# Copying a matrix with its four quadrants exchanged: one DMA per 64 rows with runs of 16 KB, in place of two with runs of 8 KB

## The chip, the cores and the metric

The kernel runs on one core of a Trainium2 chip. The metric is the device time of one execution in microseconds (us). The kernel before was timed three times: median 811.06 us, from 810.79 to 811.39.

The core has five engines with their own instruction queues (PE, DVE, ACT, POOL, SP) and 16 DMA engines that move data without them. The profile abbreviates SP's queue as SPq.

## The reference

```python
def setup_inputs():
    return {
        "x": np.random.randn(8192, 8192).astype(np.float32),
    }

def reference(x: np.ndarray) -> np.ndarray:
    return np.fft.ifftshift(x)
```

For even sizes `ifftshift` moves every element by half the matrix in both directions: `out[r, c] = x[(r + 4096) % 8192, (c + 4096) % 8192]`. The four quadrants of the matrix change places across the diagonal. Nothing is computed. A row has 8192 floats of 4 bytes, 32 KB; half a row is 16 KB and is contiguous in both matrices. The matrix has 268.4 MB, which must be read once and written once.

## The kernel before

There is no tile in the core's memory: every DMA copies straight from the input tensor in HBM to the output tensor in HBM. The helper `both` issues one such DMA on a given queue. It takes `rows` output rows from `row` on, and of each row two pieces of `piece` floats: one at column `col` in the left half, one at the same place in the right half, `hc` = 4096 floats further on. Both pieces come from the same input row, `hr` = 4096 rows away; the left piece of the output is read from the right half of the input (the middle dimension of the input pattern steps by `-hc`). So the order inside the DMA is row by row, and in each row the left piece of the output, then the right one.

The loop at the end of the function goes over the matrix in blocks of `rows = ENGINES * apart` = 64 rows. The outermost dimension of the DMA's pattern has these 64 rows, and the 16 DMA engines share them, four consecutive rows (`apart`) each. For every block there are two DMAs, one for each `col` in `(0, piece)` with `piece = hc // 2` = 2048 floats: the first copies the first 8 KB of either half of the rows, the second the last 8 KB. A DMA moves 1 MB; 128 blocks make 256 DMAs, all issued on SP's queue in the order of the loop. Within one DMA an engine has 4 rows x 2 pieces = 8 contiguous runs of 8 KB.

No two DMAs touch the same output bytes, and none reads what another wrote, so no DMA depends on another. The framework gives each DMA a semaphore that its 16 engines count up when their share has landed, and there are eight of these in turn: before it issues a DMA, SP waits until the one issued eight earlier has landed. At the end SP waits for the last ones.

Of the kernel before, what the change touches and what calls it, by code (L numbers as in the profile page):

```python
# [1 line left out]

# [4 lines left out]


ENGINES = 16  # L10


@with_exitstack
def kernel(
    ctx: ExitStack,
    tc: tile.TileContext,
    x: bass.AP,
    out: bass.AP,
):
    nc = tc.nc  # L20
    R, C = x.shape
    hr = R // 2
    hc = C // 2

    def both(queue, row, col, rows, piece):

        queue.dma_start(
            out=bass.AP(out.tensor, out.offset + row * C + col, [[C, rows], [hc, 2], [1, piece]]),
            in_=bass.AP(
                x.tensor,  # L30
                x.offset + (row + hr) % R * C + hc + col,
                [[C, rows], [-hc, 2], [1, piece]],
            ),
        )


    apart = 4
    piece = hc // 2
    rows = ENGINES * apart
    for row in range(0, R, rows):  # L40
        for col in (0, piece):
            both(nc.sync, row, col, rows, piece)


# [1 line left out]
_INS = ['x']  # L46
_OUTS = [((8192, 8192), 'float32')]


def kernel(**inputs):  # L50
    import numpy as _np
    import concourse.bacc as _bacc
    import concourse.tile as _tile
    from concourse import mybir as _mybir
    from concourse.bass_utils import run_bass_kernel_spmd as _run

    nc = _bacc.Bacc("TRN2", target_bir_lowering=False, num_devices=1)  # L57
    arrays, args = {}, []
    for name in _INS:
        a = _np.ascontiguousarray(inputs[name])  # L60
        if a.dtype.kind in "iu":
            a = a.astype(_np.int64)
        arrays[f"in_{name}_dram"] = a
        args.append(nc.dram_tensor(f"in_{name}_dram", a.shape, _mybir.dt.from_np(a.dtype), kind="ExternalInput").ap())
    for i, (shape, dtype) in enumerate(_OUTS):
        dt = _mybir.dt.from_np(_np.dtype(dtype))
        args.append(nc.dram_tensor(f"out_{i}_dram", shape, dt, kind="ExternalOutput").ap())
    with _tile.TileContext(nc) as tc:
        kernel(tc, *args)
    r = _run(nc, [arrays], core_ids=[0])  # L70
    got = tuple(r.results[0][f"out_{i}_dram"] for i in range(len(_OUTS)))
    return got[0]
```

## Time and profile before

| | |
|---|---|
| median of three runs | 811.06 us |
| the profiled execution | 810.44 us |
| its span, first to last instruction | 808.7 us |
| DMA instructions (line 27, SP) | 256 of 1024 KB |
| median time from a DMA's issue to its landing | 25.1 us (from 6.0 to 26.0) |
| time of one DMA instruction on SP | 562 ns, the longest 682 |
| first and last issue | 0.7 and 783.1 us |
| busy time of POOL, the only engine with any | 0.2 us, four memsets |

The profile comes from one execution; its time lies 0.6 us below the median of the three timed runs. Besides the page, the trace holds a record of each DMA packet: when it started, how long it took and its size, though not on which engine it ran. A rate in GB/s counts the bytes once, while each is read and written; the page's figure for HBM counts both directions.

### The profile page before, as it was taken

The page shows a single profiled execution, that of the slowest core. Times are in us where ns is not written, and L with a number is a line of the kernel's source. Part 1 is how long each engine was busy: PE and PEld are TensorE (multiplying, and loading weights), DVE is VectorE, ACT ScalarE, POOL GpSimd, SP SyncE. Part 2 cuts the span into 40 slices and gives each one's busy share as a digit, 9 for nine tenths or more (in the row PEclk, how much of TensorE's full clock was granted, in tenths as well). Part 3 has the DMA queues.
Part 4 walks back from the last instruction along what each step waited for, and adds up shares of the span by engine and source line. Part 5 has one row for each costly group of instructions (what it writes and reads, how often), then busy time and mean ns, then how long its engine had stood idle before and what let it go on. Part 6 is the DMA issues. An engine that isn't in the chain of part 4 may idle for free. (4 is left out here: it accounts for less than half of the span.)

```text
span 808.7 us, 301 instructions
## 1 busy us (share of the span) xinstructions
POOL 0.2 (0%) x4
## 2 busy tenths in 40 slices
POOL 0000000000000000000000000000000000000000
DMA  8999999999999999999999999999999999999998
GB/s 301 331 335 329 336 334 330 335 332 336 332 335 334 336 331 334 339 328 335 331 335 339 334 334 337 331 336 330 336 334 331 339 332 334 333 336 331 337 335 294
DMA packets 36866, 268.47 MB, mean 332 GB/s; under 512 B 4096, under 2 KB 4096, under 8 KB 4096
## 3 DMA queue, kind: packets, MB, share of 16 engines
q1 hardware_dynamic: 36864, 268.45, 99.3%
q14 instruction: 2, 0.02, 0.0%
HBM read 268.44 MB, written 268.44 MB: 664 GB/s over the span
## 5 line engine op out<-in xcount | busy, mean ns | idle before, releaser
L57 POOL MEMSET const-bfloat16-1.0<- 128x1 bf16 x1 | 0.1, 102 | 0.0
L57 POOL MEMSET const-uint8-127<- 128x1 uint8 x1 | 0.1, 102 | 0.0
L57 POOL MEMSET const-float32-1.0<- 128x1 f32 x1 | 0.1, 99 | 0.0
L57 POOL MEMSET const-float32-0.0<- 128x1 f32 x1 | 0.1, 98 | 0.2 <-issue 0.2
## 6 DMA issues: line engine op xcount, KB each, us to landing
out_dram<-in_x_dram SPq DMA_DIRECT2D x256, 1024.0 KB, 25.1
```

The costliest lines, as they stand in the source:

```text
L57: nc = _bacc.Bacc("TRN2", target_bir_lowering=False, num_devices=1)
```

## The change

The loop over the two column pieces goes away. Each block of 64 rows is copied by one DMA whose pieces are the whole halves: `col` is 0 and `piece` is `hc` = 4096 floats. A contiguous run is 16 KB in place of 8 KB, a DMA moves 2 MB in place of 1 MB, and there are 128 DMAs in place of 256. The number of runs that an engine has in one DMA stays at eight, and so do the order of rows and halves, the queue, the rows that an engine takes and the eight semaphores.

```diff
     apart = 4
-    piece = hc // 2
     rows = ENGINES * apart
     for row in range(0, R, rows):
-        for col in (0, piece):
-            both(nc.sync, row, col, rows, piece)
+        both(nc.sync, row, 0, rows, hc)
```

## The prediction

> **What bounds the kernel now.** I read the page's queue table first, then SP's waits, then the busy table of chosen stretches of the span, and last the single packet records of the trace (start, length and size of each). No compute engine does anything but four memsets at the start, and the chain of waits ends with them after 0.4 us, so it says nothing here: everything is in the DMA queue.
>
> ```profile
> span 808.7 us, 301 instructions
> ...
> DMA packets 36866, 268.47 MB, mean 332 GB/s; under 512 B 4096, under 2 KB 4096, under 8 KB 4096
> ## 3 DMA queue, kind: packets, MB, share of 16 engines
> q1 hardware_dynamic: 36864, 268.45, 99.3%
> q14 instruction: 2, 0.02, 0.0%
> HBM read 268.44 MB, written 268.44 MB: 664 GB/s over the span
> ```
>
> Of 36,864 packets 4,096 are under 512 B: 16 for each of 256 DMAs, the semaphore packets (4 B in the records). The other 32,768 carry 268.44 MB, 8192 B each, one contiguous run of the code. Their time fills 99.3% of the 16 engines: no engine idles for want of work. SP confirms it:
>
> ```profile
> SPq L27 <- DMA out_dram<-in_x_dram: 634.0, 248, 3.2
> ```
>
> 256 DMAs less 248 waits: SP keeps 8 in flight and waits for the oldest before each further one. So the issue is no limit. The question left is whether the engines or the memory behind them set the pace:
>
> ```profile
> core 0: us, POOL busy (x), PEclk, DMA share, GB/s
> 4.00:5.40 1.40, 0.00 (x0) 1.00 1.03 433
> 8.00:12.00 4.00, 0.00 (x0) 1.00 1.01 344
> 20.00:780.00 760.00, 0.00 (x0) 1.00 1.00 334
> 804.00:805.40 1.40, 0.00 (x0) 1.00 0.99 404
> ```
>
> The last column is what one direction moved. The same engines, as busy as later, moved 433 GB/s in the first DMA, 344 a little later and 334 for the rest. They can do more than they are let do, and what holds them back builds up within microseconds. In the packet records the shortest usual packet takes 309 ns, and on its engine the next begins 3 to 4 ns before it ends: a period of 306 ns, or 428 GB/s for 16 engines, the rate of the first DMA. From 20 us on, 62% of the packets take this floor; the mean is 391 ns. Summed, an engine's data packets take 800.8 us, of which 168 us lie above the floor. I call that part stall. The limit is shared, behind the engines, and shows as stall.
>
> Is stall tied to the packet boundary? By following each engine's chain of packets (matched by their times, so a few links may be wrong) I get the mean stall by place in a DMA, packets 1 to 8 (four rows, right half of the input then left): 91, 73, 77, 86, 90, 75, 76, 88 ns. The first packet behind a semaphore is no worse than the others, so there is no cost per DMA. But 1, 4, 5 and 8 average 88.7 and the others 75.3: which half of which row is read matters to the memory. And stall is not independent from packet to packet: behind an unstalled packet the mean is 105 ns, behind one stalled by 300 to 500 ns it is 14. While one packet is held, the next, of the other half, comes in.
>
> **The change, part by part.** The profiled execution took 810.44 us, 0.62 under the median 811.06. It consists of 2.18 us to the first packet, 805.35 to the end of the last, 1.13 to the end of the span, and 1.78 outside it. The change issues 128 DMAs in place of 256, each an engine's 8 data packets of 16 KB instead of 8 KB, over the same rows in the same order; bytes are the same.
>
> Issue: 128 DMA instructions fewer on SP (median 562 ns each), and 120 waits in place of 248. SP has no other work. I cost this at nothing: the 7 DMAs queued behind the one that runs hide it, and they now hold twice the bytes. Without that cover the saving would be on the path, at most 128 x 0.56 = 72 us; the 99.3% rules that out. Landing should go from 25.1 to about 50 us, which delays nobody.
>
> Fixed cost of packets: the nearest row is the semaphore packet, 4 B, 9 ns with 3 ns overlapped, so 6 ns for almost no data. Each engine has 1024 data and 128 semaphore packets fewer: 1152 x 6 = 6.9 us at most. At least it is nothing, if the memory hands out its bytes at 334 GB/s whatever the engines spare. As a majority of packets runs at the engine's floor, but the total is held at 334, I take half: -3.5 us.
>
> The Trainium skill ("DMA: Bandwidth & Descriptors", section "Why small descriptors are slow") gives a packet about 3 cycles of fixed overhead inside the engine and counts it as important for packets of 256 B; by it, at the 850 MHz of its bandwidth section, the data packets save 1024 x 3.5 ns = 3.6 us where engines set the pace. The trace's 6 ns agrees in kind.
>
> End: the engines' last packets end between 805.5 and 807.5 us. Twice the granule can stretch that by as much again; 0 to +2 us, I take +1.
>
> Stall: an engine now stays 612 ns instead of 306 in one half before it alternates. The trace has no 16 KB packet, so I bound the term. Upper end: the relief by a neighbour from the other half is gone, and each 8 KB is stalled like one behind an unstalled packet: (105 - 82) x 2048 packets = +47 us. Lower end: longer runs suit the memory and all packets come down to the better places: (75.3 - 82) x 2048 = -13.7 us. The nearest row is the spread by place, +-6.7 ns or +-13.7 us, since what doubles is the stay in one place. I give it the positive sign, as held packets are now relieved by the other half only after 16 KB; and half its size, because reading ahead goes on. That it goes on can be seen at the start: a first packet took 1058 ns, 749 over the floor, the next 309 at once, so at 306 ns a packet about 2.4 packets (20 KB) were already under way. This reach covers 2.4 packets now and 1.2 of 16 KB. Term taken: +6.9 us.
>
> Sum: 810.44 - 3.5 + 1 + 6.9 = 814.8 us; against the median, 811.06 + 4.4 = 815.5.
>
> **Rivals.** *No change.* The memory sets 334 GB/s whatever the run length: 811, from 809.4 to 812.7 (0.2% either way is about what a measurement here can tell). For it: the flat rate in the 38 inner slices of the page (328 to 339), and no stall tied to the boundary. Against it: stall depends on half and neighbour, which the change touches. If the hardware cuts a run of 16 KB into packets of 8 KB, the change does not do what it says and also ends here, at most 0.8 us (128 semaphore packets) faster.
>
> *Faster.* Each 16 KB block is now visited once, where before its second 8 KB came a DMA (3.1 us) later. If stall per byte stays as it is, the whole 6.9 us show: 804.2. If in addition the memory keeps the 344 GB/s of the stretch from 8 to 12 us, 268.4 MB take 780 instead of 804 us: 787. For it: 344 and 433 were reached. Against: it was lost again by 20 us with no change in the code's pattern.
> "HBM Reference" of the Trainium skill (section "Specifications (TRN2)") gives 716 GB/s for the stack; by it this copy of 537 MB could not end under 750 us, an estimate, and the 664 of the page leaves 7%. The first DMA's 2 x 433 lies above that figure for 1.4 us.
>
> *Much slower.* If not even the next packet of 16 KB can be read ahead, each pays its latency: 612 + 749 = 1361 ns, x 1024 = 1394 us, some 1399 in all. The point from which it decides: with one packet read ahead a period would be 749 ns, 350 GB/s, still over 334, so it decides only when reading ahead holds less than one full packet. Against it: the 20 KB under way seen above.
> One rule speaks for it: the Trainium skill's "DMA: Bandwidth & Descriptors" ("Latency and other measured facts", on row pitch) has HBM to HBM copies of rows of 16 KiB at 214 GB/s a direction at best. By it the copy would take 1254 us, about 1259 with the ends; this trace, at 8 KB, moves 334, and none here shows 16 KB.
>
> **Chances.** Forecast, somewhat slower (over 812.7): 0.44. No change: 0.14. Faster (under 809.4): 0.37, of which about 0.07 lies below 793. Much slower: 0.05. Predicted time 815.5. Cases of both signs hold most of the chance: the forecast's own range is 812.7 to 845 (0.05 of the forecast's case lies above, towards +47). The range 793 to 845 leaves out 0.07 + 0.05 + 0.05. Faster 0.37, same 0.14, slower 0.44 + 0.05 = 0.49.
>
> **What would show it.** 16,384 data packets and 2,048 semaphore packets on the queue; floor about 610 ns (two floors less one fixed cost); under 35% of the packets at the floor (35% of today's pairs of neighbours have no stall) and a mean over 2 x 391 = 782 ns; GB/s between 20 and 780 us about 331; SP's waits 120. A mean under 776 ns shows the faster rival, first packets far over 1.4 us that repeat later the much slower one. Wrong would be the sign above all: if both 8 KB halves of a block are cheap together for the memory, the stall term is negative.

## The result and the profile after

The changed kernel takes 814.01 us (median of 6 runs, 813.39 to 814.80). The kernel before took 810.90 us in the 6 runs of the same comparison. The ratio is 1.0038, 95% interval 1.0027 to 1.0048: slower by 3.1 us, where 4.4 were forecast. The profiled execution took 813.94 us.

First the queue table of the changed kernel:

```profile
span 812.2 us, 173 instructions
...
DMA packets 18433, 268.45 MB, mean 331 GB/s; under 512 B 2048, under 2 KB 2048, under 8 KB 2048
## 3 DMA queue, kind: packets, MB, share of 16 engines
q1 hardware_dynamic: 18432, 268.44, 99.5%
...
HBM read 268.44 MB, written 268.44 MB: 661 GB/s over the span
```

2,048 semaphore packets and 16,384 data packets, so a run of 16 KB is one packet, and the rival in which it is cut does not hold. The engines are as full as before (99.5%). They are full for longer.

SP's waits (for whom, us in total, times, longest):

```profile
SPq L27 <- DMA out_dram<-in_x_dram: 686.8, 120, 6.8
SPq L66 <- DMA out_dram<-in_x_dram: 49.0, 4, 31.0
```

120 waits, on average 5.7 us where 2.6 were before; the median landing went from 25.1 to 50.5 us. As reckoned, that idles no engine: the engines stay full.

The stretches, in the same columns as in the prediction (the last is GB/s in one direction):

```profile
core 0: us, POOL busy (x), PEclk, DMA share, GB/s
4.00:5.40 1.40, 0.00 (x0) 1.00 1.00 386
8.00:12.00 4.00, 0.00 (x0) 1.00 1.00 340
20.00:780.00 760.00, 0.00 (x0) 1.00 1.00 332
804.00:805.40 1.40, 0.00 (x0) 1.00 0.98 328
```

Here the time went: 332 in place of 334 GB/s over the long middle. That is 0.6%, to be read with its rounding; on 804 us it would be 3 to 5 us. By the packet records the middle 96% of the bytes take 3.2 us longer, so the ends hardly matter.

The packet records say what an engine's 807.0 us of data packets are made of. The floor is 611 ns for 16 KB, where two packets of 8 KB took 618; the mean is 788 ns, where two took 782. Above the floor lie 181.4 us an engine in place of 168.0. So the floors fell by 7 us of packet time, and stall rose by 13. Not all of the 7 us is engine time: each packet still begins 3 to 4 ns before the one ahead of it ends, so one data packet fewer spares its engine some 3.6 ns and not 7, 3.7 us in all. The experiments ask what these numbers mean.

### The profile page after: what moved, and what is told of

It is laid out like the page before. It is cut to its first block, busy times and chain, and to the rows that moved or that the text cites. A ratio compares the mean times of both kernels' runs of the same rounds, so it can differ in the third digit from the quotient of the medians.

```text
span 812.2 us, 173 instructions
## 1 busy us (share of the span) xinstructions
POOL 0.2 (0%) x4
## 2 busy tenths in 40 slices
DMA packets 18433, 268.45 MB, mean 331 GB/s; under 512 B 2048, under 2 KB 2048, under 8 KB 2048
## 3 DMA queue, kind: packets, MB, share of 16 engines
q1 hardware_dynamic: 18432, 268.44, 99.5%
## 6 DMA issues: line engine op xcount, KB each, us to landing
out_dram<-in_x_dram SPq DMA_DIRECT2D x128, 2048.0 KB, 50.5
```

## The experiments

The first four ran on a chip on which the kernel before takes 823.5 us, the later ones on two chips with 810.5 and 811.1. Ratios are to the kernel before on the same chip, with 95% intervals. The expectations speak of three theories: S (the engine's stay in one half of a row makes the stall), W (the size of a DMA does) and P (the length of a packet does).

**16 KB runs in small DMAs.** One row for each engine, 512 KB, 512 DMAs; each engine copies the same runs in the same order as in the changed kernel. (The trace does not say on which engine a packet ran; which rows an engine takes is read from the access pattern.)

```diff
-        both(nc.sync, row, 0, rows, hc)
+        for one in range(apart):
+            both(nc.sync, row + one, [apart * C, ENGINES], hc)
```

(The helper takes the outermost dimension in place of a number of rows.)

> 16 KB runs as in the changed kernel, each engine with the same runs in the same order, but 512 DMAs of 512 KB (one row an engine) in place of 128 of 2 MB, so 4 MB in flight in place of 16. Theory S (the engine's stay in one half of a row, 16 KB, makes the stall): the DMA's size does not matter, about 814 us plus 384 more semaphore packets an engine at 6 ns, up to 2.3 us: 814 to 817. Rival W (the larger DMA, its 16 MB in flight or its coarser end cost the 3 us): 811 or under, with the stall per 16 KB back from 177 ns to about 164. Rival P (the packet's length itself): as S, 814 to 817.

Measured: 823.71 us, 1.0001 (0.9991 to 1.0011). As a ratio, that is what W expected, and under the range of S and P.

**The changed kernel's order in packets of 8 KB.** 128 DMAs of 2 MB; of each half the second 8 KB first, then the first.

```diff
-    out [[C, rows], [hc, 2], [1, piece]]   in [[C, rows], [-hc, 2], [1, piece]]
+    out [[C, rows], [hc, 2], [-piece, 2], [1, piece]]   in [[C, rows], [-hc, 2], [-piece, 2], [1, piece]]
```

(Shorthand: the access patterns alone. `piece` is 4096 floats in the first line and 2048 in the second, where both sides also start `piece` further on.)

> The changed kernel's 128 DMAs of 2 MB and its stay of 16 KB in one half of a row, but in two packets of 8 KB (the second 8 KB of a half first, so that the runs are not joined). Theory S (stay in one half): the stall of the changed kernel and the fixed cost of 1024 more packets an engine, 814 plus 0 to 6 us: 814 to 820. Rival P (a packet of 16 KB, whatever its place): 810 to 812, as before. Rival W (size of the DMA): 814.

Measured: 824.18 us, 1.0005 (0.9997 to 1.0014). As a ratio, that is what P expected; S and W expected about 1.004 or more.

**Alternating packets of 8 KB in DMAs of 2 MB.** The kernel before with `apart = 8`.

> Packets of 8 KB that alternate between the halves as in the kernel before, but DMAs of 2 MB (128 rows, 8 rows to an engine), so 16 MB in flight as in the changed kernel. Theory S and rival P: 810 to 811.5, as before, the 128 semaphore packets fewer worth at most 0.8 us. Rival W: about 814. The engines stand 8 rows apart in place of 4, which none of the theories counts.

Measured: 823.04 us, 0.9991 (0.9982 to 1.0000). That fits S and P and not W. It is 1.1 us less than the run before, which has the same packets and the same size of DMA in the changed order.

**Alternating packets of 4 KB.** The kernel before with `piece = hc // 4` and four columns.

> Packets of 4 KB that alternate between the halves, 512 DMAs of 512 KB. Theory S: half the stay of the kernel before, so stall per byte goes down by about as much as it rose from 8 to 16 KB (13 us), against the fixed cost of 2048 more data and 256 more semaphore packets an engine at 6 ns, 13.8 us if all of it shows: 798 to 812. Rival P: the fixed cost alone, 811 to 825. Rival W: smaller DMAs, 808 to 811.

Measured: 845.58 us, 1.0257 (1.0232 to 1.0282), 22 us slower. All three expectations failed. The stretches of this kernel:

```profile
8.00:12.00 4.00, 0.00 (x0) 1.00 1.08 231
12.00:20.00 8.00, 0.00 (x0) 1.00 1.02 276
20.00:40.00 20.00, 0.00 (x0) 1.00 1.03 300
40.00:60.00 20.00, 0.00 (x0) 1.00 1.03 308
60.00:100.00 40.00, 0.00 (x0) 1.00 1.02 325
```

A slump at the start, which takes until 60 us to pass, and then 322 to 325 GB/s up to 780 us, where the 8 KB kernels of this chip have 328 and 329. So a shorter stay in one half is not better in itself, or its gain is smaller than what 4 KB costs; the two can't be told apart here.

The first three contradict each other: one fits W alone, one P alone, one S and P. What they say stayed unclear, because the changed kernel had not run on that chip, and packets are held longer on it. The floor of a packet is the same there, but the alternating 8 KB packets of 2 MB DMAs have a mean of 398.3 ns, and 393.5 on one of the other chips. So the changed kernel was run again beside two of them.

**The changed kernel again**, on the chip with 810.5 us.

> The changed kernel once more, beside the two below on one chip, since the former experiments ran on a chip on which the kernel before takes 823.5 us and not 811. If the 0.38% belong to the kernel, the ratio is again 1.003 to 1.005; if they belong to the first chip, 0.999 to 1.001. Theories S and P say the first, and so does W.

Measured: 814.11 us, 1.0035 (1.0022 to 1.0047). The loss is there on a second chip, so it is the kernel's.

**16 KB runs in small DMAs, again.**

> 16 KB runs in 512 DMAs of 512 KB once more, now beside the changed kernel. Theories S and P: like the changed kernel, within 0.1% of it. Rival W (16 MB in flight make the difference): like the kernel before, ratio 0.999 to 1.001, with the changed kernel at 1.003 to 1.005.

Measured: 812.47 us, 1.0017 (1.0006 to 1.0027), between the theories: a smaller loss than the changed kernel's, despite 384 more semaphore packets for each engine. On one chip, with the same runs in the same order on each engine, the size of the DMA alone moves the time by 1.6 us (814.11 to 812.47).

**The changed order in packets of 8 KB, again.**

> The changed kernel's order and DMAs, its 16 KB in two packets of 8 KB, once more, now beside the changed kernel. Theory S: like the changed kernel, ratio 1.003 to 1.006. Rival P: like the kernel before, 0.999 to 1.001.

Measured: 814.67 us, 1.0041 (1.0027 to 1.0056). From the page of this kernel, and its long stretch:

```profile
DMA packets 34817, 268.45 MB, mean 330 GB/s; under 512 B 2048, under 2 KB 2048, under 8 KB 2048
```

```profile
20.00:780.00 760.00, 0.00 (x0) 1.00 1.00 332
```

34,817 packets less 2,048 semaphore packets and one of instructions are 32,768 of 8 KB. This speaks strongly against rival P. Packets of 8 KB, floor 309 ns, and a loss as large as the changed kernel's is there. It needs no packet of 16 KB; the order of the bytes or the size of the DMA is enough for it. (Within a half the second 8 KB now comes first, which no theory counts, so this run does not show what the changed kernel's own order costs in packets of 8 KB.)

**The kernel before again**, for its trace on this chip.

> The kernel before, for a profile of it on the chip of these runs: ratio 1, and if the chip's memory is what differs from the first chip, the same floor of 309 ns and a higher mean than 391 ns.

Measured: 810.14 us in one run, mean packet 391.7 ns at the same floor, as on the first chip (391). Its stretch:

```profile
20.00:780.00 760.00, 0.00 (x0) 1.00 1.00 334
```

Against it the 8 KB kernel with the changed order has 4.2 us more stall an engine (177.6 against 173.4, both counted from 307 ns) with equal packets. This surplus is no sign of the order: the next run alternates like the kernel before, in DMAs of 2 MB, and has 177.3.

**Alternating 8 KB in DMAs of 2 MB, again**, on the chip with 811.1 us, as the last three.

> Packets of 8 KB that alternate between the halves, in DMAs of 2 MB over 128 rows, once more, to compare with the runs on a chip where the kernel before takes 811 us. Rival W (DMAs of 2 MB, 16 MB in flight): ratio 1.003 to 1.005, like the changed kernel. Theory S (two stretches of 8 KB of one half in succession, in one packet or in two): 0.999 to 1.001, like the kernel before. If the chip is again the one of 823 us, 0.998 to 1.000 as there, and W is then weaker by one more run only.

Measured: 812.26 us, 1.0016 (1.0007 to 1.0024). Neither expectation: DMAs of 2 MB have a part of the loss, about 0.16 of the 0.4%. Its stretch:

```profile
20.00:780.00 760.00, 0.00 (x0) 1.00 1.00 333
```

Where that part comes from is open; the run also sets the engines 8 rows apart.

**16 KB runs in DMAs of 1 MB.** The changed kernel with `apart = 2`.

> 16 KB runs, left and right half in succession, in DMAs of 1 MB as in the kernel before (32 rows, engines 2 rows apart in place of 4). Rival W: 0.999 to 1.001. Theory S: 1.003 to 1.005. Between them, 1.001 to 1.003, if both have a part, as the 512 KB DMAs with 1.0017 let suspect.

Measured: 813.75 us, 1.0035 (1.0023 to 1.0047). A DMA as large as in the kernel before, and all of the loss. By itself it speaks for S and against W.

**Alternating 8 KB in DMAs of 512 KB.** The kernel before with `apart = 2`, the control of the run above.

> Packets of 8 KB that alternate between the halves, in DMAs of 512 KB (32 rows, engines 2 rows apart), so 4 MB in flight in place of 8. Rival W: less in flight is better, so 0.996 to 0.999 less the 256 more semaphore packets (up to 1.5 us): 0.996 to 1.001. Theory S: 1.000 to 1.002, the semaphore packets alone. It is also the control for the engines' distance of the run before it.

Measured: 813.42 us, 1.0027 (1.0016 to 1.0038). Above S's range, and it weakens the run before it: at 2 rows apart, 8 KB runs lose too. 256 more semaphore packets at 6 ns would be 1.5 us of its 2.2, if all of it showed. Beside this control the 16 KB runs cost 0.08% more, less than the intervals can tell. Less in flight does not help, which is against W. The trace can't say where the time went, since the profiled execution was the fastest of the seven (811.11 us) and as quick as the kernel before:

```profile
20.00:780.00 760.00, 0.00 (x0) 1.00 1.00 334
```

**16 KB runs, one half per DMA.** An engine copies four left halves, then four right halves.

```diff
-        both(nc.sync, row, 0, rows, hc)
+        for half in (0, hc):
+            one(nc.sync, row, half, rows)
```

> 16 KB runs, but a DMA of 1 MB takes the left half of 64 rows and the next the right half: an engine copies four left halves, then four right halves. If the relief comes from the other half of the row (theory S as the prediction has it), an engine now stays four packets in one half: 1.006 or more. If only the two stretches of 8 KB in succession count, 1.003 to 1.005. Rival W (DMA of 1 MB): 0.999 to 1.001.

Measured: 819.12 us, 1.0107 (1.0084 to 1.0130), as theory S said. But its trace says when:

```profile
8.00:12.00 4.00, 0.00 (x0) 1.00 0.92 291
...
20.00:210.00 190.00, 0.00 (x0) 1.00 1.00 324
210.00:400.00 190.00, 0.00 (x0) 1.00 1.00 330
400.00:590.00 190.00, 0.00 (x0) 1.00 1.00 332
590.00:780.00 190.00, 0.00 (x0) 1.00 1.00 332
```

The kernel loses in the first 400 us, most of it in the first 200. From 400 us on it has 332 GB/s, no less than the changed kernel. A plausible reading is that the engines, which start together in the same half, drift apart and then cover both halves among them; the runs did not test it. What the trace shows is that a stay of four packets costs nothing beyond that of one from 400 us on.

The runs of 8 and 16 KB together, as ratios:

| | packets | DMA | engines apart | chip of 823.5 us | chips of 810.5 and 811.1 us |
|---|---|---|---|---|---|
| changed kernel | 16 KB | 2 MB | 4 rows | not run | 1.0035 |
| its runs in small DMAs | 16 KB | 512 KB | 4 rows | 1.0001 | 1.0017 |
| its runs in DMAs of 1 MB | 16 KB | 1 MB | 2 rows | not run | 1.0035 |
| changed order | 8 KB | 2 MB | 4 rows | 1.0005 | 1.0041 |
| alternating | 8 KB | 2 MB | 8 rows | 0.9991 | 1.0016 |
| alternating | 8 KB | 512 KB | 2 rows | not run | 1.0027 |
| one half per DMA | 16 KB | 1 MB | 4 rows | not run | 1.0107 |

No single theory fits them all. In DMAs of 2 MB the changed order costs more than alternation, by 1.1 us on one chip and by some 2 us between the others; the size of the DMA moves the time by about as much (1.6 us with 16 KB runs, 1.3 us with alternating 8 KB). The distance of the engines changed along with the size of the DMA in three of the runs and was never varied alone, so it is a rival that stands untested. The three kernels that ran on both kinds of chip lose 0.16 to 0.36% less on the slow one, and why is open too. None of the kernels is faster than the one before beyond the intervals.

## Why the prediction came out, and where its terms were wrong

The sign, the size and the place were right: somewhat slower, 0.38% against a forecast of 0.54%, through a rate in the middle of 332 against a forecast of 331 (by the prediction's own sum it should have said nearly 333). The marks were met: 120 waits, a floor of 611 ns (about 610), 32% of the packets at it (under 35), a mean of 788 ns (over 782). The bound was read rightly: the memory's pace, not the engines'. That the sum came so near is in part luck. The prediction itself gave slower 0.49 and faster 0.37, and the errors of its terms cancel: counted in engine time, both the saving (3.5) and the stall (6.9) were too small, as the traces have 9 to 10 and 13.4 us; counted in what the kernel's time shows, both were too large.

**What bounds the kernel.** Borne out. The slower chip has the same floor and more stall, so what differs between the chips lies behind the engines; and twice as many packets for the same bytes did not cost time, as the point on fixed cost shows.

**Issue, nothing.** Right. The landings doubled and the engines stayed at 99.5%.

**Fixed cost of packets, -3.5 us.** Wrong in size, and this is the step that failed most clearly. The price was too high: a data packet fewer spared its engine 3.6 ns (618 - 611 = 7 less the lost overlap) and not 6. And the time did not show even that. The changed kernel and the same order in packets of 8 KB, on one chip, differ by 1024 data packets an engine and by 0.6 us (814.11 and 814.67); the ratios 1.0035 and 1.0041 carry some 0.0013 each, so up to about 2 us may hide there, 3.5 hardly. Their traces (profiled executions of 814.65 and 814.67 us) show the exchange: the kernel with 8 KB packets spends about 4 us more of an engine on fixed cost and 5 more in gaps, has 9 us less stall (173.5 against 182.9), and from the first packet to the last both take 809.5 us. "If the memory hands out its bytes at 334 GB/s whatever the engines spare", the lower end, was the nearer one: what an engine spared came back as stall. The prediction had the evidence (16 engines that could move 428 and are let move 334) and still took half.

**End, +1 us.** No such cost was found. The last packets end within 1.6 us, where 2.0 were before (1.4 and 1.1 in the traces of the chip with 810.5 us). In its place stands a cost of the 2 MB DMAs that the prediction did not have: 1.3 us by the run with alternating 8 KB (0.6 to 1.9), in the steady rate (333 against 334, to be read with the rounding) and not at the end. Its cause is open, and the smaller DMAs do not line up with it: the 16 KB runs lose least at 512 KB, the 8 KB runs lose at 512 KB too, with the engines 2 rows apart.

**Stall, +6.9 us.** Right in sign, wrong in size, and its reason is not shown. The changed order in DMAs of 2 MB, at equal packets, costs 3.3 us (1.0041); less the 1.3 of the large DMAs some 2.0 are left for the order, with an uncertainty of about 1.5, from runs on two chips. The pair on the chip with 823.5 us gives 1.1. The 13 us by which stall rose are mostly the engines' savings given back as waiting: about 5 us of fixed cost (data and semaphore packets, less the lost overlaps) and 4.6 us less of gaps between packets (8.3 to 3.7 us an engine, by the chains). What is left, about 4 us, is the time that the kernel lost (3.5 us from the first packet to the last in these two traces). And the row that the size was taken from, the spread by place in a DMA, does not carry over: in the changed kernel the places 1, 4, 5 and 8 average about 177 ns of stall, and 2, 3, 6 and 7 about as much. That an engine is relieved by the other half stays unproved: four packets in one half ran at 332 like one, from 400 us on. Whether it is the alternation that helps, or the return to a block a DMA later, was not separated. An order of 8 KB packets that alternates and comes back two packets later was not tried.

**The rivals.** Much slower: excluded, 16 KB packets are read ahead (an unstalled packet lasts 611 ns, and 32% do). The rule of the Trainium skill ("DMA: Bandwidth & Descriptors", "Latency and other measured facts"), 214 GB/s a direction at best for HBM to HBM copies of 16 KiB rows, was measured with rows 512 KiB and more apart and does not carry over to this copy, whose rows lie 32 KB apart: 332. Faster: stall per byte did not stay as it was, and the 344 GB/s were again lost by 20 us (340 between 8 and 12 us). No change: the flat rate that spoke for it was real, but the rate itself moved, from 334 to 332.

## What to carry to other kernels

When 16 busy DMA engines together move less than their own floor allows, do not expect fewer or longer packets to pay: here the time saved in the engine reappeared as stall (the changed kernel and its order in twice as many packets took 814.1 and 814.7 us). The shortest packet and the rate of the first microseconds tell the two limits apart. To learn whether a longer run or its order costs, cut the long run into short packets and keep the order as far as the pattern allows; here that run had the whole loss without the long packet. And run the changed kernel beside the experiments on the same chip: without it the first three runs here could not be read.

## What the runs showed of the hardware

- Two chips of the same kind differ by 1.5% on this copy (medians of the kernel before, 823.5 us against 810.5 and 811.1), more than any of the orders of 8 and 16 KB tried moved it (1.1% at most).
- With 16 data packets for each engine in a DMA, SP did not wait for landings inside the loop (line 27) at all; the DMA instruction itself took long. Its only waits for DMAs in the run of alternating 8 KB in 2 MB DMAs come at the end:

```profile
SPq L68 <- DMA out_dram<-in_x_dram: 35.8, 4, 17.8
```

  The times of one DMA instruction (least, median, most) in that run, and in the changed kernel, which has 8 data packets in a DMA of the same size:

```profile
L27 SPq DMA_DIRECT2D out_dram<-in_x_dram x128: 600/5851/14306, 0.7 to 767.4; - x128
```

```profile
L27 SPq DMA_DIRECT2D out_dram<-in_x_dram x128: 562/562/692, 0.7 to 761.6; - x128
```

  Landing took 41.9 us there, not 50.5. At 6.3 us a DMA that is 6.7 DMAs, or some 113 packets of an engine in flight (an estimate from these numbers), fewer than the eight that the semaphores allow, so something else holds SP back; what it is was not tested.
- Packets of 4 KB cost 22 us (on the chip with 823.5 us), more than the 14 us that 6 ns for each additional packet would make, with a slump to 231 GB/s at the start.
